# A hybrid decoder layer on one core: transposes one at a time inside the columns, a step more for two chains, and norms' sums kept in written order

## The chip, the core and the metric

The kernel runs on one core of a Trainium2 chip. The metric is device microseconds of one execution. The core's engines work side by side, each through its own instructions in order: PE (TensorE: matmuls, and transposes, which are matmuls with the identity), ACT (ScalarE), DVE (VectorE), POOL (GpSimd) and SP (SyncE). POOL and SP serve here mostly as queues that start DMA transfers. An instruction that waits for another engine holds up everything behind it on its own engine.

## The reference, cut to what matters

The input is 2048 tokens by 1024. One layer is computed in float32:

```
h    = rmsnorm(x) * w1
proj = h @ w_in                       # 3840 columns: 2048 for HGRN2, 1792 for RWKV-7
o_hg = HGRN2 recurrence, 4 heads of 128, each head normed by its mean square, then gated
o_rw = RWKV-7 recurrence, 8 heads of 64 (state S <- S*w + (S a) b' + v k'), group norm, gate
x    = x + concat(o_hg, o_rw) @ w_out
x    = x + conv_ffn(rmsnorm(x) * w2)  # up 1024 -> 5632, causal conv of 3, SiLU gate, down
out  = rmsnorm(x) * w_final
```

## The kernel before

The program has two parts. Part 1 (`phase1`) makes the input projection, both recurrences and most of the output projection; part 2 makes the feed-forward network and the final norm. Every large matmul is made three times on operands split into a high and a low half (L270 to L272, tile `pj` in part 1). What stands in part 2 is not touched here.

Part 1 is written as three Python generators that are advanced in turn:

- `rw_stream` goes through eight RWKV supers (`rw_super`: one block of 512 tokens, two pairs of heads). In a super, PE makes the products of keys and receptances (L730), DVE takes them into `M`, a DMA turns them round through DRAM into `E`, and DVE then solves 31 dependent rows (L802 and L804) and transposes the result into `TZ` (L808). Only then can PE go on: L821, L834 and L847 complete the inverse, ACT copies L847's result out into `UV` and `M`, L867 and L881 prepare the states, and eight steps of L905 and L910 carry the state through the block. A group norm ends the super.
- `hg_stream` goes through sixteen HGRN units (`hg_unit`: one block, one head). At a unit's end PE makes the output (L1064 and L1065), ACT squares it and makes its high half, DVE the low half (`part`), and PE sums both halves over the head (`add_up`, L1083 and L1084, tile `hg`).
- `dense` makes the projection: 30 columns of 128 outputs per block, each of 8 steps k of three matmuls into one of two PSUM banks (`pj`). At a column's end its function takes the result out of the bank: for HGRN one ACT and at most one DVE instruction, for RWKV one ACT and three DVE (L313 to L315). Between columns stand jobs: `load4` loads four rows' tiles (`xt`, one buffer) by SP, `norm4` computes their norm on ACT (`nsq`: squares and sums; `nst`: logarithm and exponential) and DVE, and a transposing job turns the 8 slices of 128 features. Job "T" (`turn`) does so for the next block of x, three times in all; job "N" for block 0 and 1 of the first residual, for the second norm, and stores to `h2d` in DRAM. Each transposed slice takes a `pj` bank, and ACT empties it. `sum_load` and `sum_make` form sums of blocks of `h2d` (`four_sums`, L240 to L243) for part 2; `o_take` brings in halves of an output block. `out_block` makes the output projection of a block.

The pace is set by `fill`: in each round the two streams make one step (to their next `yield`), and then `dense` is advanced for as many nanoseconds, by its own yields, as the constant allows:

```
TICK = 2000.0
        while any(alive.values()):
            for key, g in (("r", rw_), ("h", hg_)):
                ...
                        next(g)
            fill(TICK)
```

A step k of a column is charged 648 ns, a transposed slice 436 ns. The order that results is a priority. A scheduler then places the instructions on each engine by it and by when it reckons that inputs are there and banks are free, so an instruction can stand earlier or later than written. Weights are split while they arrive and kept in DRAM (`Win`) for the later blocks.

Of the kernel before, what the change touches and what calls it, by code (L numbers as in the profile page):

```python
# [7 lines left out]
F32 = mybir.dt.float32  # L8
# [3 lines left out]
AF = mybir.ActivationFunctionType  # L12
# [6 lines left out]
P = 128  # L19
T = 2048  # L20
D = 1024
KD = D // P
BLK = 512
# [44 lines left out]
def tile_layer(ctx, tc, consts, x, norm1_w, w_in, hg_lb_logits, hg_norm_w, rw_shift_mu, rw_w0, rw_w2,  # L68
# [4 lines left out]
    V, S, TE = nc.vector, nc.scalar, nc.tensor  # L73
    dma, store = nc.sync.dma_start, nc.gpsimd.dma_start
# [11 lines left out]
    ident = cp.tile([P, P], F32, name="ident")  # L86
# [27 lines left out]
    def act(out_, in_, func, **kw):  # L114

        want = tables.get(func)
        if want is not None and want != tab["now"]:
            pre = S.preload_act_table_set(want)
            for u_ in tab["uses"]:
                tc.add_manual_dep(pre.ins, u_.ins.name, NOSYNC, reason="table order")  # L120
            tab.update(now=want, pre=pre, uses=[])
        i_ = S.activation(out_, in_, func, **kw)  # L122
        if want is not None:
            tc.add_manual_dep(i_.ins, tab["pre"].ins.name, NOSYNC, reason="table order")
            tab["uses"].append(i_)
        return i_
# [13 lines left out]
    with tc.tile_pool(name="vp", bufs=1, reuse_waits="tile") as vp, tc.tile_pool(name="ps0", bufs=1, space=PSUM, reuse_waits="tile") as pools["ps"]:  # L140
        rows = vp.tile([P, P], F32, name="rows")
# [17 lines left out]
    def vec(nm, i):  # L159
        return vt[:, off[nm] + i:off[nm] + i + 1]  # L160
# [24 lines left out]
    x1d = [dp.tile([BLK, D], F32, name=f"x1d{b}") for b in range(NBLK)]  # L185
    h2d = [dp.tile([D, BLK], F32, name=f"h2d{b}") for b in range(NBLK)]
# [50 lines left out]

    def four_sums(b11, b12, b21, b22):

        V.tensor_sub(b11, b12, b11)  # L240
        V.tensor_sub(b12, b22, b12)
        V.tensor_sub(b22, b22, b11)
        V.tensor_sub(b21, b21, b22)  # L243
        return b11, b22, b12, b21

    def split_to(hi, lo, src):
        c_ = S.copy(hi, src)
        return c_, V.tensor_sub(lo, src, hi.bitcast(F32))
# [9 lines left out]
    def transposed(xt, nm, psum, evict):  # L258

        n = len(xt)  # L260
        for k in range(KD):
            tp = psum()
            for i in range(n):
                TE.transpose(tp[:, i * P:(i + 1) * P], xt[i][:, k * P:(k + 1) * P], ident)
            evict(k, tp[:, :n * P], vec(nm, k))
            yield 109 * n

    def mm3(acc, lhs, rhs, first, last, skip=False):
        (lh, ll), (rh, rl) = lhs, rhs
        TE.matmul(acc, lh, rh, start=first, stop=False, skip_group_check=skip)  # L270
        TE.matmul(acc, lh, rl, start=False, stop=False, skip_group_check=skip)  # L271
        TE.matmul(acc, ll, rh, start=False, stop=last, skip_group_check=skip)  # L272

    def phase1(c1):
# [22 lines left out]
        def bank(kind):  # L297
            return ps.tile([P, 512], F32, tag=kind, name=kind, bufs=2)
# [121 lines left out]
        def load4(key, src, r0):  # L420
            def f():
                rows[key] = row_tile()
                for i in range(4):
                    dma(rows[key][:, i, :], src[r0 + i * P:r0 + (i + 1) * P, :])
            return f

        def norm4(key):
            def f():
                for i in range(4):
                    t_ = rows[key][:, i, :]  # L430
                    V.tensor_scalar_mul(t_, t_, rstd(wp, t_, "nst", "wraw", 4))
            return f

        def four_tiles(t_):
            return [t_[:, i, :] for i in range(4)]

        def turn(nb):

            t_ = rows[nb]
            for k in range(KD):  # L440
                tp = bank("pj")
                for i in range(4):
                    TE.transpose(tp[:, i * P:(i + 1) * P], t_[:, i, k * P:(k + 1) * P], ident)
                act(t_[:, :, k * P:(k + 1) * P], tp.rearrange("p (i t) -> p i t", i=4), AF.Copy)
                yield 436

        def split_h(nb, k):

# [25 lines left out]
        def o_take(m):  # L474

            def f():
                if m == 0:
                    t_ = xp_.tile([P, 2, 2, 4, 256], F32R, tag="xt", name="ohl", bufs=1)
                    rows["O"] = [[t_[:, c, i] for i in range(2)] for c in range(2)]
                t_ = wp.tile([P, 2, 256], F32, tag="wraw", name="oraw", bufs=4)  # L480
                dma(t_, oT[2][2 * m * P:2 * (m + 1) * P, 0:256].rearrange("(k p) t -> p k t", p=P))
                ks = slice(2 * (m % 2), 2 * (m % 2) + 2)
                split_to(rows["O"][0][m // 2][:, ks, :], rows["O"][1][m // 2][:, ks, :], t_)
            return f

        def to_h(k, tp, w):
            act(hh[:, k, :], tp, AF.Copy, scale=w)
            V.scalar_tensor_tensor(hl[:, k, :], tp, w, hh[:, k, :].bitcast(F32), ALU.mult, ALU.subtract)

        def to_h2(nb):  # L490
            def evict(k, tp, w):
                t_ = wp.tile([P, BLK], F32, tag="wraw", name="h2", bufs=4)
                act(t_, tp, AF.Copy, scale=w)
                dma(h2d[nb][k * P:(k + 1) * P, :], t_)
            return evict

        def constants():

# [17 lines left out]
        def dense():  # L516
# [26 lines left out]
            extra = []  # L543
            for nb in range(NBLK):
                if nb + 1 < NBLK:
                    extra += [(at[nb] + 18, ("E", load4(nb + 1, x[0], (nb + 1) * BLK))),
                              (at[nb] + 22, ("E", norm4(nb + 1))), (at[nb] + 25, ("T", nb + 1))]
                if nb >= 2:
                    extra += [(at[nb] + 6, ("E", load4(("N", nb - 2), x1d[nb - 2], 0))),
                              (at[nb] + 10, ("E", norm4(("N", nb - 2)))), (at[nb] + 11, ("N", nb - 2))]  # L550
            for m in range(2):
                extra += [(at[3] + 14 + 5 * m, ("E", sum_load(m))), (at[3] + 17 + 5 * m, ("E", sum_make(m)))]
            extra += [(at[3] + 25 + m, ("W", 2, o_take(m))) for m in range(4)]
# [24 lines left out]
            i = 0  # L578
            load(0)
            ahead = iter(())  # L580
            for n, jb in enumerate(jobs):
                if jb[0] == "E":
                    jb[1]()
                    continue
                if jb[0] == "A":
                    if jb[1] == 0:
                        banks = spread()
                        ahead = transposed(four_tiles(rows[0]), "n1", lambda: next(banks), to_h)
                    continue
                if jb[0] == "T":  # L590
                    yield from turn(jb[1])
                    continue
                if jb[0] == "N":
                    yield from transposed(four_tiles(rows.pop(jb)), "n2", lambda: bank("pj"), to_h2(jb[1]))
                    continue
                if jb[0] in "OW":
                    while done["rw2"] < 2 * jb[1] + 2 or done["hg"] < 4 * jb[1] + 4:
                        yield None
                    if jb[0] == "W":
                        jb[2]()  # L600
                    else:
                        yield from (out_block(2, *rows["O"]) if jb[1] == 2 else out_block(jb[1], then=jb[1] + 2))
                    continue
                _, col, ev, cond, fin = jb
                while not cond():
                    yield None
                load(i)
                ws = loaded.pop(i)
                if i == 0:
                    next(ahead)  # L610
                    next(ahead)
                    constants()
                load(i + 1)
                i += 1
                acc = bank("pj")
                then = jobs[n + 1][1] if jobs[n + 1][0] == "A" else None
                for k in range(KD):
                    wh, wl = ws[k // 4]
                    next(ahead, None)
                    mm3(acc, (wh[:, k % 4, :], wl[:, k % 4, :]), (hh[:, k, :], hl[:, k, :]), k == 0, k == KD - 1)  # L620
                    if k == KD - 1:
                        ev(acc)
                        if fin is not None:
                            fin()
                    next_block(then, k)
                    yield 648

        def last_dma(nb):

# [17 lines left out]
        def rw_super(nb, s_):  # L647
# [6 lines left out]
            def tile_(tag, shape, name):  # L654
                return rp.tile([P] + shape, F32, tag=tag, name=name)
# [200 lines left out]
            for e in range(2):  # L856
                r0, c0 = er0(e), col0(1, e)
                act(M[r0:r0 + 64, 0, 1, :, :, 0:64], quv[1][c0:c0 + 64, :, :, 0:64], AF.Copy)
            yield
            XH = tile_("XH", [2, 9, 64], "XH")  # L860
            V.tensor_copy(XH[:, :, 0, :], Xc[:, 2 * s_:2 * s_ + 2, :])
            xp = bank2()
# [81 lines left out]
        def hg_unit(nb, j):  # L944
# [122 lines left out]
            act(sq, op, AF.Square)  # L1067
            hi, lo = (rp.tile([P, BLK], F32R, tag=tag, name="part") for tag in ("Sf", "VT"))
            split_to(hi, lo, sq)
            yield  # L1070
            ms = bank("hg")
            add_up(ms, ones, hi, lo)
# [552 lines left out]
```

## Time and profile before

| | us |
|---|---|
| median of 3 runs (lowest, highest) | 2640.78 (2636.36, 2642.07) |
| the profiled execution | 2641.65 |
| its span, first to last instruction | 2639.9 |
| part 1, to the first matmul of the last output block, about | 1303 |
| part 2 | 1337 |
| PE busy over the span | 2551.4 |
| DVE, ACT, POOL busy | 1963.1, 1371.3, 381.4 |

The profiled execution stands 0.87 above the median, so a sum worked out against it is read against the median with that difference. Times inside the trace count from the start of the span. The listed duration of a matmul is longer than its pace: those of 512 columns are listed at 0.39 and start every 0.23, since they overlap in the array. A gap is counted from the end of the one before, so it is smaller than what was lost by some 0.16. "PEclk" is the share of the full clock that was granted to PE.

### The profile page before, as it was taken

The page shows a single profiled execution, that of the slowest core. Times are in us where ns is not written, and L with a number is a line of the kernel's source. Part 1 is how long each engine was busy: PE and PEld are TensorE (multiplying, and loading weights), DVE is VectorE, ACT ScalarE, POOL GpSimd, SP SyncE. Part 2 cuts the span into 40 slices and gives each one's busy share as a digit, 9 for nine tenths or more (in the row PEclk, how much of TensorE's full clock was granted, in tenths as well). Part 3 has the DMA queues.
Part 4 walks back from the last instruction along what each step waited for, and adds up shares of the span by engine and source line. Part 5 has one row for each costly group of instructions (what it writes and reads, how often), then busy time and mean ns, then how long its engine had stood idle before and what let it go on. Part 6 is the DMA issues. An engine that isn't in the chain of part 4 may idle for free.

```text
span 2639.9 us, 51054 instructions
## 1 busy us (share of the span) xinstructions
PE 2551.4 (97%) x19467; PEld 2046.3 (78%) x19467; DVE 1963.1 (74%) x3744; ACT 1371.3 (52%) x2258; POOL 381.4 (14%) x686
## 2 busy tenths in 40 slices
PE   7999999989999999999899999999999999999998
PEld 6877777767777767777678888877888888888887
DVE  4878676685666765777687799987998887766556
ACT  5565443555545555345466754456454544545444
POOL 6433222212222122222100000000000000000000
PEclk9999999999999999999999999999999999999999
DMA  8846463646645566845674477746763553998655
GB/s 305 240 153 193 157 176 110 149 149 216 193 168 145 158 211 187 277 145 149 204 253 134 130 235 255 235 158 217 239 207 129 174 169 132 332 321 283 200 190 187
DMA packets 380298, 518.98 MB, mean 197 GB/s; under 512 B 114463, under 2 KB 211093, under 8 KB 380053
## 3 DMA queue, kind: packets, MB, share of 16 engines
q1 hardware_dynamic: 325521, 337.38, 40.2%
q0 software_dynamic: 54464, 178.32, 21.0%
q8 instruction: 153, 2.51, 0.4%
q14 instruction: 92, 0.75, 0.1%
q10 hardware_dynamic: 68, 0.02, 0.0%
HBM read 372.99 MB, written 134.22 MB: 192 GB/s over the span
## 4 chain that ended last, share of the span: by engine, by line
PE 69%; DVE 13%; ACT 7%; DMA 7%; issue 4%; POOL 0%; SPq 0%; DVEq 0%; ACTq 0%; POOLq 0%
PE pj L270 7%; PE pj L271 7%; PE pj L272 7%; PE ua L270 4%; PE ua L272 4%; PE ua L271 4%; PE da L270 3%; PE da L271 3%; PE da L272 3%; PE ud L271 2%; PE ud L270 2%; PE ud L272 2%; PE db L272 2%; PE db L271 2%; PE db L270 2%
## 5 line engine op out<-in xcount | busy, mean ns | idle before, releaser
L270 PE MATMUL pj<-hh,wh 128*128 128x512 f32 x960 | 392.2, 409 | 4.5 <-ACT rkv L122 2.5
L271 PE MATMUL pj<-hl,wh 128*128 128x512 f32 x960 | 378.4, 394 | 0.0
L272 PE MATMUL pj<-hh,wl 128*128 128x512 f32 x960 | 378.3, 394 | 0.0
L270 PE MATMUL ua<-Bh,uwh 128*128 128x512 f32 x704 | 276.8, 393 | 3.0 <-ACT m L122 2.5
L272 PE MATMUL ua<-Bh,uwl 128*128 128x512 f32 x704 | 274.5, 390 | 0.0
L271 PE MATMUL ua<-Bl,uwh 128*128 128x512 f32 x704 | 274.2, 389 | 0.0
L270 PEld LDWEIGHTS pj<-hh,wh 128*128 128x128 f32 x960 | 181.2, 189 | 53.5 <-issue 8.3
L272 PEld LDWEIGHTS pj<-hh,wl 128*128 128x128 f32 x960 | 181.3, 189 | 39.5 <-issue 0.2
L271 PEld LDWEIGHTS pj<-hl,wh 128*128 128x128 f32 x960 | 181.3, 189 | 35.3 <-issue 0.6
L254 ACT CAST uwh<-uraw 128x512 fp32r<-128x512 f32 x220 | 134.2, 617 | 131.0 <-PE ua L271 54.0
L255 DVE TENSOR_TENSOR dal<-draw,dah 128x512 fp32r<-128x512 f32 x138 | 95.2, 690 | 110.9 <-ACT dah L254 108.5
L255 DVE TENSOR_TENSOR uwl<-uraw,uwh 128x512 fp32r<-128x512 f32 x220 | 147.1, 684 | 32.8 <-ACT uwh L254 32.7
L254 ACT CAST dah<-draw 128x512 fp32r<-128x512 f32 x138 | 85.8, 622 | 164.2 <-PE da L271 77.8
L270 PEld LDWEIGHTS ua<-Bh,uwh 128*128 128x128 f32 x704 | 132.3, 188 | 34.8 <-ACT m L122 7.0
L272 PEld LDWEIGHTS ua<-Bh,uwl 128*128 128x128 f32 x704 | 132.3, 188 | 28.1 <-DVE uwl L255 0.4
L271 PEld LDWEIGHTS ua<-Bl,uwh 128*128 128x128 f32 x704 | 132.2, 188 | 26.6
L1495 POOL DMA_DIRECT2D gd<-y x2 | 1.1, 540 | 949.0 <-DVE y L1493 949.0
L270 PE MATMUL ud<-Bh,uwh 128*128 128x512 f32 x352 | 138.0, 392 | 0.0
L272 PE MATMUL ud<-Bh,uwl 128*128 128x512 f32 x352 | 137.1, 390 | 0.0
L271 PE MATMUL ud<-Bl,uwh 128*128 128x512 f32 x352 | 137.0, 389 | 0.0
L271 PE MATMUL da<-dbl,dah 128*128 128x512 f32 x332 | 129.5, 390 | 0.2 <-DVE dbl L255 0.2
L272 PE MATMUL da<-dbh,dal 128*128 128x512 f32 x332 | 129.2, 389 | 0.0
(582 smaller groups left out, 6202.6 us busy)
## 6 DMA issues: line engine op xcount, KB each, us to landing
uraw<-in_w_up_dram SPq DMA_DIRECT2D x176, 256.0 KB, 3.2
woraw<-in_w_out_dram POOLq DMA_DIRECT2D x96, 256.0 KB, 3.6
br<-gd SPq DMA_DIRECT2D x88, 256.0 KB, 4.3
draw<-Sg SPq DMA_DIRECT2D x88, 256.0 KB, 3.0
draw<-Tw SPq DMA_DIRECT2D x88, 256.0 KB, 3.2
gd<-y SPq DMA_DIRECT2D x86, 256.0 KB, 3.0
Sg<-br SPq DMA_DIRECT2D x72, 256.0 KB, 2.5
xt<-x1d SPq DMA_DIRECT2D x32, 512.0 KB, 6.2
```

The source lines that it names most:

```text
L254: S.copy(hi, src)
L255: V.tensor_sub(lo, src, hi.bitcast(F32))
L270: TE.matmul(acc, lh, rh, start=first, stop=False, skip_group_check=skip)
L271: TE.matmul(acc, lh, rl, start=False, stop=False, skip_group_check=skip)
L272: TE.matmul(acc, ll, rh, start=False, stop=last, skip_group_check=skip)
L1495: (dma if end is None else nc.gpsimd.dma_start)(gd_[2 * h + b][fb * P:(fb + 1) * P, :], ys[0][:, b * BLK:(b + 1) * BLK])
```

## The change

Four edits, all in part 1:

1. `four_sums`: its first subtraction is tied behind whatever DVE instruction is written before it. The same is done to the two instructions of each split in `o_take`.
2. `turn` becomes a job per slice. The slices are put on a list, and a column takes one from it after its matmuls of k = 1 and one after k = 5; the step that does so is charged 648 + 436. For the next block the slices are spread one per column over eight columns (from column 22), for the second norm two per column over four (`turn2`, from column 8). The loads and norms ahead of them move to column 17 and 20 (before 18 and 22), and 4 and 7 (before 6 and 10).
3. `rw_super` has one `yield` more between ACT's copies out of L847 and the states (L867).
4. `hg_unit` has one more between the split and the sum (L1083).

```diff
-        V.tensor_sub(b11, b12, b11)
+        tc.keep_in_program_order(V.tensor_sub(b11, b12, b11))
...
-        def turn(nb):
-
-            t_ = rows[nb]
-            for k in range(KD):
+        def turn(nb, k):
+
+            def f():
+                t_ = rows[nb]
                 tp = bank("pj")
                 for i in range(4):
                     TE.transpose(tp[:, i * P:(i + 1) * P], t_[:, i, k * P:(k + 1) * P], ident)
                 act(t_[:, :, k * P:(k + 1) * P], tp.rearrange("p (i t) -> p i t", i=4), AF.Copy)
-                yield 436
+            return f
+
+        def turn2(key, k):
...
+                h2 = wp.tile([P, BLK], F32, tag="wraw", name="h2", bufs=4)
+                act(h2, tp, AF.Copy, scale=vec("n2", k))
+                dma(h2d[key[1]][k * P:(k + 1) * P, :], h2)
...
-                split_to(rows["O"][0][m // 2][:, ks, :], rows["O"][1][m // 2][:, ks, :], t_)
+                for i_ in split_to(rows["O"][0][m // 2][:, ks, :], rows["O"][1][m // 2][:, ks, :], t_):
+                    tc.keep_in_program_order(i_)
...
-                    extra += [(at[nb] + 18, ("E", load4(nb + 1, x[0], (nb + 1) * BLK))),
-                              (at[nb] + 22, ("E", norm4(nb + 1))), (at[nb] + 25, ("T", nb + 1))]
+                    extra += [(at[nb] + 17, ("E", load4(nb + 1, x[0], (nb + 1) * BLK))),
+                              (at[nb] + 20, ("E", norm4(nb + 1)))]
+                    extra += [(at[nb] + 22 + k, ("T", turn(nb + 1, k))) for k in range(KD)]
                 if nb >= 2:
-                    extra += [(at[nb] + 6, ("E", load4(("N", nb - 2), x1d[nb - 2], 0))),
-                              (at[nb] + 10, ("E", norm4(("N", nb - 2)))), (at[nb] + 11, ("N", nb - 2))]
+                    extra += [(at[nb] + 4, ("E", load4(("N", nb - 2), x1d[nb - 2], 0))),
+                              (at[nb] + 7, ("E", norm4(("N", nb - 2))))]
+                    extra += [(at[nb] + 8 + k // 2, ("T", turn2(("N", nb - 2), k))) for k in range(KD)]
...
                 if jb[0] == "T":
-                    yield from turn(jb[1])
+                    turns.append(jb[1])
                     continue
...
                     mm3(acc, (wh[:, k % 4, :], wl[:, k % 4, :]), (hh[:, k, :], hl[:, k, :]), k == 0, k == KD - 1)
+                    aside = k in (1, 5) and len(turns) > 0
+                    if aside:
+                        turns.pop(0)()
...
-                    yield 648
+                    yield 648 + 436 * aside
...
                 act(M[r0:r0 + 64, 0, 1, :, :, 0:64], quv[1][c0:c0 + 64, :, :, 0:64], AF.Copy)
             yield
+            yield
             XH = tile_("XH", [2, 9, 64], "XH")
...
             split_to(hi, lo, sq)
             yield
+            yield
             ms = bank("hg")
             add_up(ms, ones, hi, lo)
```

In the changed kernel, lines of `rw_super` stand 9 or 10 further down (L821 is L830, L867 is L877), those of `hg_unit` 10 or 11 (L1083 is L1094). How the order moves at three places:

PE where block 2 of x is transposed, at about 490 us (L443 are the transposes of x, a row's `x12` is three slices; L1083 and L1084 are the sums of RWKV's norms). Before:

```order
L272 MATMUL pj<-hh,wl 128x512
L443 MATMUL pj<-ident,xt 128x128 x12
L1083 MATMUL rw<-part,group 128x512
L443 MATMUL pj<-ident,xt 128x128 x12
L1084 MATMUL rw<-part,group 128x512
L1083 MATMUL rw<-part,group 128x512
L1084 MATMUL rw<-part,group 128x512
L443 MATMUL pj<-ident,xt 128x128 x8
L270 MATMUL pj<-hh,wh 128x512
```

And one of the eight slices now:

```order
L270 MATMUL pj<-hh,wh 128x512
L271 MATMUL pj<-hl,wh 128x512
L272 MATMUL pj<-hh,wl 128x512
L443 MATMUL pj<-ident,xt 128x128 x4
L1094 MATMUL rw<-part,group 128x512
L1095 MATMUL rw<-part,group 128x512
L1094 MATMUL rw<-part,group 128x512
L1095 MATMUL rw<-part,group 128x512
L270 MATMUL pj<-hh,wh 128x512
```

The eight slices stood in one run with only the sums between; now each stands alone between a column's matmuls.

DVE in block 3, where the second of the two `four_sums` stood (L240 to L243, tile `xt`; the rest are HGRN's levels and norm, and L887 is RWKV's, for which L881's second half waits). Before:

```order
L1076 TENSOR_TENSOR osq<-hg,osq 128x512
L240 TENSOR_TENSOR xt<-xt 128x1024
L1077 TENSOR_TENSOR hgg<-osq,hgg 128x512
L947 TENSOR_SCALAR hk<-hf 128x512
L974 TENSOR_TENSOR hf<-hf 128x256
L971 TENSOR_TENSOR hX<-hk,Sf 128x128x2
L965 TENSOR_TENSOR hX<-hq,hf 128x128x2
L972 TENSOR_TENSOR Sf<-Sf,hf 128x128x2
L241 TENSOR_TENSOR xt<-xt 128x1024
```

Now the first `four_sums` stands at this place, whole, and the second one comes only after all eight state steps:

```order
L240 TENSOR_TENSOR xt<-xt 128x1024
L241 TENSOR_TENSOR xt<-xt 128x1024
L242 TENSOR_TENSOR xt<-xt 128x1024
L243 TENSOR_TENSOR xt<-xt 128x1024
L968 MEMSET Sf 128x256
L313 SCALAR_TENSOR_TENSOR rkv_13102<-pj,vt,rkv_13102 128x511
L1087 TENSOR_TENSOR osq<-hg,osq 128x512
```

The sums moved as a group, and none is left ahead of RWKV's additions.

ACT at the start of block 2 (and, alike, of block 3), where the second norm's rows are squared as they arrive (`nsq`) and the first columns' results are taken out (`tl`, `rkv`). Before:

```order
L122 ACTIVATE nsq,nst<-xt 128x1024
L122 ACTIVATE tl<-pj,omu 128x512
L122 ACTIVATE nsq,nst<-xt 128x1024
L122 ACTIVATE tl<-tl 64x512
L122 ACTIVATE nsq,nst<-xt 128x1024 x2
L122 ACTIVATE rkv_7891<-pj,omu 128x512 x2
L122 ACTIVATE rkv_7966<-pj,omu 128x512
```

Now:

```order
L122 ACTIVATE tl<-tl 64x512
L118 ACT_TABLE_LOAD
L122 ACTIVATE nst<-nst,eps_71 128x1 x2
L122 ACTIVATE nst<-nst 128x1
L122 ACTIVATE nsq,nst<-xt 128x1024
L122 ACTIVATE nst<-nst 128x1
L122 ACTIVATE rkv_7895<-pj,omu 128x512
L122 ACTIVATE nst<-nst,eps_71 128x1
L122 ACTIVATE nsq,nst<-xt 128x1024
```

The first RWKV result is now taken out before the fourth square instead of after it, and the norm's logarithm and exponential, with a load of ACT's function table, came in between. The order has 61 such loads in the whole program where it had 53; those of part 2 are the same. From the last matmuls of part 1 on, PE, DVE and ACT have the same instructions in the same order as before.

More of the change, by code (lines that the diff above doesn't have):

```diff
@@ L444, in turn, with f @@
                 act(t_[:, :, k * P:(k + 1) * P], tp.rearrange("p (i t) -> p i t", i=4), AF.Copy)
-                yield 436
+            return f
+        def turn2(key, k):
+            def f():
+                t_ = rows[key]
+                tp = bank("pj")
+                for i in range(4):
+                    TE.transpose(tp[:, i * P:(i + 1) * P], t_[:, i, k * P:(k + 1) * P], ident)
+                h2 = wp.tile([P, BLK], F32, tag="wraw", name="h2", bufs=4)
+                act(h2, tp, AF.Copy, scale=vec("n2", k))
+                dma(h2d[key[1]][k * P:(k + 1) * P, :], h2)
+            return f
         def split_h(nb, k):
@@ L488, in to_h @@
             V.scalar_tensor_tensor(hl[:, k, :], tp, w, hh[:, k, :].bitcast(F32), ALU.mult, ALU.subtract)
[L490 to L495, printed above, removed]
         def constants():
@@ L580, in dense @@
             ahead = iter(())
+            turns = []
             for n, jb in enumerate(jobs):
@@ L590, in dense @@
                 if jb[0] == "T":
-                    yield from turn(jb[1])
-                    continue
-                if jb[0] == "N":
-                    yield from transposed(four_tiles(rows.pop(jb)), "n2", lambda: bank("pj"), to_h2(jb[1]))
+                    turns.append(jb[1])
                     continue
```

## The prediction

> **What bounds the kernel now.** I read the page's engine totals first, then the two parts as windows of their own, PE's waits, the places where its clock fell, and the timeline around each of the four edits.
>
> ```profile
> span 2639.9 us, 51054 instructions
> PE 2551.4 (97%) x19467; PEld 2046.3 (78%) x19467; DVE 1963.1 (74%) x3744; ACT 1371.3 (52%) x2258; POOL 381.4 (14%) x686
> ```
>
> The windows' columns are length, busy time of PE, PE's weight loads, DVE, ACT and POOL (instructions), PE's clock, DMA share, GB/s. The first is part 1, the second part 2.
>
> ```profile
> 0.00:1303.00 1303.00, 1233.67 (x13666) 965.09 (x13667) 906.91 (x2148) 663.95 (x1116) 365.54 (x657) 0.99 0.60 182
> 1303.00:2640.00 1337.00, 1317.73 (x5803) 1081.24 (x5802) 1056.21 (x1597) 707.30 (x1143) 15.81 (x29) 1.00 0.64 210
> ```
>
> PE is the bound in both, and the work on it is the same after the change. Part 2 keeps its order, so the change can reach only the 1303.00 − 1233.67 = 69.3 us in which PE stands in part 1, the clock there, and new waits. The waits that the edits touch (engine, line, releaser: us in all, times, longest):
>
> ```profile
> PE hg L1084 <- DVE part L248: 5.3, 8, 1.8
> PE rw L881 <- DVE AR L887: 4.2, 1, 4.2
> PE rw L867 <- ACT M L122: 4.1, 7, 2.1
> PE pj L443 <- ACT hf L122: 4.1, 2, 2.1
> ...
> PE rw L821 <- DVE TZ L808: 2.9, 5, 1.0
> ```
>
> Together they are 20.6 of PE's 69 us. The clock adds to it: in four windows of 3.4 us it was 0.50, each at or within about 2 us behind one of these waits, so each cost half of 3.4 = 1.7 us more. A fifth window, behind a wait of 2.52, had the full clock.
>
> ```profile
> 214.90:218.30 3.40, 3.40 (x14) 2.90 (x14) 3.40 (x4) 2.87 (x7) 1.91 (x4) 0.50 0.67 227
> 416.30:419.70 3.40, 3.40 (x9) 2.31 (x7) 0.98 (x3) 3.28 (x7) 0.19 (x1) 0.50 0.50 159
> 761.00:764.40 3.40, 3.30 (x55) 3.14 (x57) 3.23 (x9) 1.80 (x4) 0.00 (x0) 0.50 0.02 5
> 1109.20:1112.60 3.40, 3.40 (x23) 2.30 (x14) 1.92 (x4) 0.07 (x1) 1.07 (x2) 0.50 0.44 161
> 987.00:990.40 3.40, 3.38 (x15) 2.81 (x16) 0.85 (x3) 0.00 (x0) 0.31 (x1) 1.00 0.13 53
> ```
>
> There is a second bound in places. Summed over the eight windows in which DVE solves RWKV's 31 rows (L802 to L808), DVE is busy 223.72 of 241.20 us, 93%, and PE arrives at L821 within a microsecond of DVE's transpose in most of them. The seventh:
>
> ```profile
> sum 241.20, PE 229.62 PEld 183.34 DVE 223.72 ACT 124.43 POOL 65.94; mean PE 28.70 PEld 22.92 DVE 27.96 ACT 15.55 POOL 8.24
> 1085.77 1.03 DVE L808 STREAM_TRANSPOSE TZ<-Ti 128x512 f32<-128x512 f32 x1
> 1086.85 0.75 PE L821 MATMUL rw<-TZ,M 32*32 32x32 f32 x64 [0.74 <-DVE TZ L808]
> ```
>
> So PE's time saved inside such a window may come back as a wait at L821; time saved outside it counts.
>
> **The change part by part.** Bounds stand in brackets, gains negative, all against the profiled 2641.65.
>
> *HGRN's extra step.* The sum (L1083, L1084) moves later on PE, past about 2 us more of matmuls by the order; nothing is added. The largest case now:
>
> ```profile
> 414.15 0.50 PE L1084 MATMUL hg<-part,ones 128*128 128x512 f32 x1 [1.84 <-DVE part L248]
> ...
> 415.29 0.75 PE L821 MATMUL rw<-TZ,M 32*32 32x32 f32 x64
> ```
>
> This gap is real, since nothing holds L821 behind it, and the drop at 416.30 follows it: 1.84 + 1.7 = 3.5. The other seven waits are 5.3 − 1.84 = 3.5 together; several lie in DVE's windows and two units still have little ahead of the sum, so I count none of them. **−3.5** [0 if later work only waits in its stead; −7.0 with all waits and the drop]. Its HGRN head ends some 2 us later; its store and the output projection that needs it stand far behind.
>
> *RWKV's extra step.* PE's work between L847 and L867 grows from about 2.5 us to 2.7 to 4.6 by the order. What is waited for is ACT's copies:
>
> ```profile
> 760.42 1.82 ACT L122 ACTIVATE M<-rw 128x512 f32<-128x512 f32 x3
> 761.07 3.85 PE L867 MATMUL rw<-UV,KBT 128*64 128x64 f32 x64 [2.06 <-ACT M L122]
> ```
>
> All of L867's 4.1 and the drop at 761.00, 1.7, are 5.8; a unit with only 2.7 of cover keeps some of its wait. **−5** [0; −5.8].
>
> *The sums in written order.* Now one `four_sums`, begun early, is spread over the state's preparation, and its third instruction stands ahead of what L881 needs:
>
> ```profile
> 1105.70 1.22 DVE L242 TENSOR_TENSOR xt<-xt 128x1024 f32<-128x1024 f32 x1
> ...
> 1107.43 0.68 DVE L887 TENSOR_TENSOR AR<-rw,AR 128x512 f32<-128x512 f32 x1
> ...
> 1108.26 0.69 PE L881 MATMUL rw<-M 64*64 64x64 f32 x32 [4.17 <-DVE AR L887]
> ```
>
> With no sum left there the wait of 4.17 and the drop at 1109.20, 1.7, go. DVE has no other instruction longer than these at this place; what is late next is the second `four_sums`, 4 × 1.22 = 4.9 us of DVE at the super's end (a rival below). **−5.5** [0; −5.9]. `o_take` orders splits whose readers come blocks of work later: nothing, hidden by the columns.
>
> *The second norm earlier.* At block 3's start ACT squares the last row, just arrived, ahead of the first RWKV result (the order above), and PE waits for that:
>
> ```profile
> 985.14 1.25 ACT L122 ACTIVATE rkv<-pj,omu 128x512 f32<-128x512 f32 x2
> 987.02 0.47 PE L270 MATMUL pj<-hh,wh 128*128 128x512 f32 x1 [2.52 <-ACT rkv L122]
> ```
>
> Now that result is taken out first, but a table load and the norm's short instructions have come in ahead of it. **−1.5** [−2.5 for the whole wait; +2.6 for two loads in the open, row below].
>
> *The transposes.* Five runs of 32 transposes become 40 slices among columns. Two runs from first transpose to next column:
>
> ```profile
> 210.96 0.60 PE L443 MATMUL pj<-ident,xt 128*128 128x128 f32 x4
> 213.54 0.66 PE L443 MATMUL pj<-ident,xt 128*128 128x128 f32 x4 [1.98 <-ACT hf L122]
> ...
> 220.84 0.50 PE L270 MATMUL pj<-hh,wh 128*128 128x512 f32 x1 [0.20 <-ACT xt L122]
> 489.68 0.60 PE L443 MATMUL pj<-ident,xt 128*128 128x128 f32 x4
> ...
> 498.11 0.50 PE L270 MATMUL pj<-hh,wh 128*128 128x512 f32 x1 [0.25 <-ACT xt L122]
> ```
>
> Needed are 32 × 0.13 (eight in 1.04 us where they ran freely) + 4 sums × 0.23 = 5.1. The first run took 9.9, the second 8.4: 4.8 (1.7 of it the clock's) and 3.3 lost. The other three I put at 2.5 each: 15.6 in all to be had. Against it stands what a slice waits inside a column. A slice needs the bank that the column before used, and it comes behind as little as six matmuls of the next, 6 × 0.23 = 1.4 us. What empties that bank (us in all, mean ns; then idle time ahead), and ACT's table load:
>
> ```profile
> L118 ACT ACT_TABLE_LOAD x53 | 68.0, 1283 | 1.7 <-PEq L1610 0.7
> L122 ACT ACTIVATE rkv<-pj,omu 128x512 f32<-128x512 f32 x48 | 32.8, 685 | 130.5 <-PE pj L272 130.4
> L313 DVE SCALAR_TENSOR_TENSOR rkv<-pj,vt,rkv 128x511 f32<-128x511 f32 x48 | 35.8, 747 | 57.8 <-ACT rkv L122 57.5
> ```
>
> Behind an RWKV column that is 0.69 + 2 or 3 × 0.75, about 2.5 us, so 1.1 more than the six matmuls cover; behind an ACT-only column 0.6 to 1.1, covered. By the order 8 slices stand behind an RWKV column, 11 behind one with two instructions, 13 behind ACT alone and 8 behind another slice, most with more than six matmuls between. My estimate of the mean waits, 0.6, 0.35, 0.2 and 0.27 for the four kinds, gives 4.8 + 3.9 + 2.6 + 2.2 = 13.5, about 14 with ends. Net **−2** [−15.6 if all is covered; 32 × 1.1 − 15.6 = +19.6 if each of the first three kinds waits like the worst].
>
> *DVE's windows and SP.* By the order's instructions at the trace's mean durations, both DVE's and PE's work inside the eight windows falls by some 7 us, so their balance stays. In two supers a store of `h2d` now stands on SP between the stores and loads that turn `M` round, and waits for a slice: some 1.5 us each at worst outside cover. **+1** [−3; +5].
>
> *Table loads.* Eight more, 8 × 1.283 = 10.3 us of ACT, which is busy half of the time, so most is hidden; a quarter in the open is **+2.5** [0; +10.3].
>
> Sum: −3.5 − 5 − 5.5 − 1.5 − 2 + 1 + 2.5 = −14.0, so 2641.65 − 14.0 = **2627.6**. The median stands 0.87 lower than the profiled run, which is inside what I can tell: no change is anything within 0.2%, 5.3 us, so 2635.5 to 2646.
>
> **The rivals.**
>
> *DVE's loop keeps its length.* If the 31 rows last as long as before with 7 us less PE work beside them, PE waits 7 more at L821; the two SP stores cost 3 rather than 1; half of the HGRN gain lies there and goes, 1.7. −14.0 + 7 + 2 + 1.7 = −3.3: 2638.4, no change to tell. For it speaks the 93% and the near ties at L821; against it, that the DVE work taken out stands in the same queue as the rows, and should shorten the loop.
>
> *The clock drops stay.* The wait of 2.52 us that ends at 987.02 had no drop behind it, so a drop isn't tied to a wait's length alone. With those at 214.90, 416.30 and 761.00 kept or put elsewhere, 3 × 1.7 = 5.1 are not gained: 2632.7. [...]
>
> *The slices wait for their banks.* If ACT and DVE have a queue at the columns' ends, 32 slices wait 1.1 as behind the worst column, 35 instead of 14, +21; and the gaps, forty short ones, drop the clock four times more, +6.8. 2627.6 + 27.8 = 2655.4, slower. It decides once the mean wait of a slice is over 0.7 us, 28 in 40: then the edits' other gains are used up. For it: two banks only, and DVE busy 93% in the windows in which some of the slices fall. Against: the order leaves 1.4 to 5.9 us of matmuls ahead of each. [...] No drop in this trace stands in a run of columns without a longer gap, so I give it no more.
>
> *The second `four_sums` blocks the super's end.* Its 4.9 us of DVE ahead of RWKV's norm reach PE: 2632.5. Against: HGRN's columns and units stand there for PE.
>
> **How the numbers follow.** My case 0.53, DVE's loop 0.18, the clock 0.08, the slices 0.15, the second sum 0.06. My case's own range is 2618 to 2635, the root of the squares of the terms' spreads on the side of their likelier ends, about 8. The range goes to 2613, where the transposes reach their good end (13.6 further), and to 2645, which takes in the loop's rival and a slice wait of 0.7 and leaves out most of the slower one: **2613 to 2645**. Faster by over 0.2%: 0.53 + 0.08 + 0.06, 0.67; within: 0.18 and a little of the others, 0.19; slower: 0.14.
>
> **What the profile after would show.** Right: no wait at L877 (L867 before), L1095's (L1084) down to about 2 us, none of 4 us at the states of block 3; no run of transposes with gaps of 2 us; waits of L443 and L453 and of the columns behind them near 14 us; at most one window at 0.50. Wrong: those waits at 28 or more; L830's (L821) at 8 or more instead of 2.9; ACT's table loads as releasers of PE's waits.

## The result and the profile after

Median of the change 2636.65 us, of the kernel before 2642.06, 20 runs each; ratio 0.9978 (0.9971 to 0.9986). One of the change's 20 runs took 4858.63 us; it counts as slow and is not in the ratio. The change is 5 to 6 us faster, 3.7 to 7.7 by the interval. The prediction was 13 faster. Its time stood in the range and its sign was right, but less than half of the gain came.

The change's page:

```profile
span 2637.6 us, 51053 instructions
PE 2545.3 (97%) x19467; PEld 2046.8 (78%) x19467; DVE 1968.2 (75%) x3744; ACT 1384.5 (52%) x2266; POOL 381.7 (14%) x686
```

Its two parts as windows, columns as before:

```profile
0.00:1301.00 1301.00, 1227.62 (x13666) 962.53 (x13667) 911.88 (x2148) 675.59 (x1124) 365.56 (x657) 0.99 0.60 183
1301.00:2637.60 1336.60, 1317.72 (x5802) 1084.23 (x5802) 1056.29 (x1597) 708.87 (x1143) 16.14 (x30) 0.99 0.64 210
```

Part 1 is 2 us shorter, and part 2 as long as before. In part 1 PE is busy 6 us less for the same number of matmuls (why is not worked out here), but it stands 73.4 us (1301.00 − 1227.62) where it stood 69.3. The waits that the edits aimed at did go. PE's waits in part 1, of the change (L1095 was L1084, L877 was L867, L891 was L881, L830 was L821, L1094 was L1083; L1000 and L1075, before L990 and L1065, are HGRN's products; L443 and L453 are the slices):

```profile
PE hg L1000 <- issue: 3.9, 3, 1.5
...
PE rw L830 <- DVE TZ L817: 3.6, 4, 1.1
PE rw L891 <- DVE AR L897: 3.4, 4, 1.3
...
PE hg L1075 <- DVE SH L1067: 3.3, 3, 1.7
...
PE hg L1000 <- DVE hk L957: 2.1, 1, 2.1
...
PE pj L270 <- ACT nsq L122: 1.7, 1, 1.7
...
PE rw L877 <- ACT M L122: 1.6, 3, 1.3
PE pj L270 <- ACT xt L122: 1.5, 1, 1.5
...
PE pj L443 <- DVE hgg L370: 1.5, 1, 1.5
PE hg L1094 <- ACT part L247: 1.3, 1, 1.3
...
PE pj L453 <- ACT h L122: 0.8, 2, 0.4
PE pj L453 <- DVE hq L346: 0.7, 2, 0.4
...
PE hg L1095 <- DVE part L248: 0.2, 1, 0.2
PE pj L443 <- DVE hq L346: 0.2, 1, 0.2
```

HGRN's sum went from 5.3 to 0.2 (its first matmul waits 1.3, before 0.4), the states from 4.1 to 1.6, the single wait of 4.2 became four short ones, and the 40 slices with the column behind one of them wait 4.7 in all (1.5 + 1.5 + 0.8 + 0.7 + 0.2). So time came back at places that the prediction had not priced. HGRN's own products are one: L1000 waits 6.0 us where L990 waited 0.3, L1075 3.3 where L1065 waited 1.3. Two more are plain in the trace. One is the fourth super's DVE loop, at about 524 us, here before and after:

```profile
524.10:559.10 35.00, 30.69 (x404) 23.88 (x402) 30.85 (x110) 19.11 (x35) 6.08 (x11) 1.00 0.56 158
```

```profile
523.70:565.50 41.80, 32.83 (x433) 25.84 (x432) 35.16 (x116) 22.81 (x40) 5.36 (x10) 0.91 0.59 157
```

The other is the crossing into part 2, whose first matmuls (`wacc`) take the last output block. PE and then DVE in the change:

```profile
1298.33 0.39 PE L272 MATMUL pj<-wh,hl 128*128 128x512 f32 x1
1300.87 1.36 PE L1281 MATMUL wacc<-woh,Bh 128*128 128x512 f32 x4 [2.15 <-ACT Bh L247]
1302.67 2.08 PE L1281 MATMUL wacc<-wol,Bh 128*128 128x512 f32 x4 [0.44 <-DVE wol L248]
1308.36 2.07 PE L1281 MATMUL wacc<-woh,Bl 128*128 128x512 f32 x4 [3.61 <-DVE Bl L248]
1300.14 0.68 DVE L1088 TENSOR_TENSOR hgg<-osq,hgg 128x512 f32<-128x512 f32 x1
...
1307.61 0.69 DVE L248 TENSOR_TENSOR Bl<-uraw,Bh 128x512 fp32r<-128x512 f32 x1 [5.00 <-DMA oT<-hgg]
```

The window behind the first of these waits:

```profile
1301.70:1311.90 10.20, 6.15 (x14) 3.98 (x13) 5.20 (x10) 3.47 (x7) 1.44 (x3) 0.50 0.88 299
```

The last HGRN product (`hgg`) is made about 1.5 us after PE had run out of matmuls, and is finished 2 us after. It goes through DRAM, and PE waits 6.2 us in three pieces; the third, 3.61, is for this way. The first ends when both the product and ACT's first `Bh` are done, within 0.01 us of each other, so the trace cannot tell which of them it was. The clock stands at 0.50 for 10.2 us. Before, the product was made 4 us ahead of PE's last columns' end, and the one wait over a microsecond there was 2.14, at full clock:

```profile
1298.16 0.68 DVE L1077 TENSOR_TENSOR hgg<-osq,hgg 128x512 f32<-128x512 f32 x1
...
1301.48 1.22 DVE L938 TENSOR_TENSOR yo<-rw,yo 128x1024 f32<-128x1024 f32 x1
1302.89 1.17 PE L1270 MATMUL wacc<-woh,Bh 128*128 128x512 f32 x4
...
1311.97 0.50 PE L1270 MATMUL wacc<-woh,Bl 128*128 128x512 f32 x1 [2.14 <-DVE Bl L248]
```

From the first `wacc` on the order is the same in both kernels, but not just ahead of it. On DVE `hgg` stood ahead of RWKV's last addition (`yo`, L938); now it stands behind it (L948, at 1299.01).

### The profile page after: what moved, and what is told of

Read it like the earlier page. It is cut to its first block, busy times and chain, and to the rows that moved or that the text cites. A ratio compares the mean times of both kernels' runs of the same rounds, so it can differ in the third digit from the quotient of the medians.

```text
span 2637.6 us, 51053 instructions
## 1 busy us (share of the span) xinstructions
PE 2545.3 (97%) x19467; PEld 2046.8 (78%) x19467; DVE 1968.2 (75%) x3744; ACT 1384.5 (52%) x2266; POOL 381.7 (14%) x686
## 4 chain that ended last, share of the span: by engine, by line
PE 53%; issue 7%; DVE 6%; DMA 5%; ACT 4%; POOL 1%; SPq 0%; DVEq 0%; POOLq 0%; ACTq 0%
PE ua L270 5%; PE ua L272 5%; PE ua L271 5%; PE pj L270 3%; PE da L271 3%; PE da L270 3%; PE da L272 3%; PE ud L271 3%; PE pj L271 3%; PE ud L270 3%; PE ud L272 3%; PE pj L272 3%; PE db L271 2%; PE db L272 2%; PE db L270 2%
```

## The experiments

Each kernel is compared with runs of the kernel before on the same chip. Differences in us are the ratio's, on 2641.

**Each edit by itself.** Four kernels, each with the kernel before and one edit's lines of the diff.

> Only the transposes are taken into the columns (with the loads and norms ahead of them); the other three edits are left out. Theory 1 (the missing gain was lost in the DVE loop of super 4 and in clock drops that the slices bring there): about 2645, +2 to +6 against before, with a lower mean clock than before. Rival 2 (the four terms are true and the loss comes only when all four stand together): the prediction's term alone, -2, so about 2640. Rival 3 (each edit deals the order anew, and what it gains at its own place is noise beside that): anything from -8 to +8, with no sum that fits.

> Only HGRN's extra step. Theory 1 and rival 2: -3.5 (0 to -7), PE's waits at the sum's second matmul down from 5.3 to about 2 us and the drop at 416 us gone. Rival 3: the waits go, and the time moves by some other number of either sign, since windows elsewhere change.

> Only RWKV's extra step. Theory 1 and rival 2: -5 (0 to -5.8), the waits at the first product of the states down from 4.1 to under 1 us. Rival 3: the waits go, the time moves by another number.

> Only the sums and the output splits in written order. Theory 1 and rival 2: -5.5 (0 to -5.9), the wait of 4.17 us in block 3 and the drop behind it gone. Rival 3: the wait goes, the time moves by another number.

| | median | ratio (95%) | us |
|---|---|---|---|
| slices, with the norms ahead of them | 2637.60 | 0.9987 (0.9977 to 0.9997) | −3.4 |
| HGRN's step | 2648.61 | 1.0029 (1.0017 to 1.0040) | +7.7 |
| RWKV's step | 2644.14 | 1.0011 (1.0000 to 1.0021) | +2.9 |
| sums in written order | 2632.10 | 0.9968 (0.9957 to 0.9980) | −8.5 |

By the ratio the sums alone do better than all four edits together, though the two intervals meet. Their trace runs beside that of before until 1085 us, and then, in block 3, the states' preparation has no wait:

```profile
1100.63 0.69 DVE L885 TENSOR_TENSOR M<-rw,cst 128x512 f32<-128x512 f32 x1 [1.43 <-PE rw L882]
1101.24 0.68 DVE L888 TENSOR_TENSOR AR<-rw,AR 128x512 f32<-128x512 f32 x1
1101.98 0.75 DVE L313 SCALAR_TENSOR_TENSOR rkv<-pj,vt,rkv 128x511 f32<-128x511 f32 x1
...
1103.76 0.69 DVE L885 TENSOR_TENSOR M<-rw,cst 128x512 f32<-128x512 f32 x1 [0.71 <-PE rw L882]
```

DVE now waits for PE where PE waited 4.17 us for DVE, and no cold window (a stretch with PE's clock at 0.50) follows.

The two steps, alone, are no gain. With HGRN's step its own sum's wait fell as foreseen, but RWKV's norm, which uses the same two lines (tile `rw`), waited instead:

```profile
PE rw L1084 <- ACT part L247: 6.8, 7, 2.0
...
PE rw L1085 <- DVE part L248: 3.4, 4, 1.4
...
PE hg L1085 <- DVE part L248: 0.9, 1, 0.9
```

10.2 us, where before the two had 2.0 and 2.6. In the first two blocks every second HGRN unit's sum stands 11 to 13 us later than before (at 206.9 for 195.6, 350.6 for 337.8), where RWKV's sums around it are 2 to 6 later. So it comes nearer to those of RWKV's norm sums that wait, at 216 to 219 and at 361. With RWKV's step the states' wait fell from 4.1 to 0.8 and the time did not fall. In the slices' trace the wait that the sums cause grew from 4.17 to 6.76, so part of the slices' gain may have been hidden behind it; the two edits together, below, do not bear this out.

Theory 1, that the slices cost, fell. Rival 2 held for slices and sums and not for the steps.

**Is it the round, or the later sum?** An extra step gives a unit one round more. So the round was given without the later sum, and the later sum without the round:

```diff
+            yield                 # ahead of the sum (hgrn_moved) ...
             ms = bank("hg")
...
             done["hg"] += 1
-            yield                 # ... and one less at the unit's end
```

`hgrn_end_step` instead has a second `yield` after that line; `rwkv_moved` has RWKV's step and none at its super's end; `sums_slices` has two edits of the change whole.

> HGRN's extra step ahead of the sum as in the change, but the step at the unit's end is taken out, so that a unit has as many steps, and the streams as many rounds, as before. Theory P (the extra step costs by its round: 16 rounds more shift the streams against the columns everywhere, and the new meetings cost more than the sum gains): the waits at the sum go and the time is -3.5 against before, 2636 to 2640. Rival L (the later sum itself costs: HGRN's norm and what follows it comes late): as with the extra step, +5 to +8, so 2647 to 2650.

> No step ahead of the sum; instead one step more at the end of each HGRN unit, where nothing waits, so the streams have the same 16 rounds more. Theory P: slower like the extra step itself and by its lost gain more, +5 to +12. Rival L: no change, -2 to +2.

> RWKV's extra step ahead of the states, and the step at the super's end taken out, so the steps of a super are as many as before. Theory P: -3 to -6 (the prediction's -5 without the price of eight rounds). Rival L: as with the extra step, +2.

> The sums in written order and the slices in the columns, without the two extra steps. If the edits add up: -9.9 and -4.3 of the single runs, so about -14 at best, 2627 to 2631, and faster than all four together by 6 or more. Rival (the edits take the same time away): 2632 to 2637, no faster than the sums alone.

| | median | ratio (95%) | us |
|---|---|---|---|
| `hgrn_moved` | 2653.28 | 1.0052 (1.0033 to 1.0071) | +13.7 |
| `hgrn_end_step` | 2640.69 | 0.9999 (0.9988 to 1.0009) | −0.3 |
| `rwkv_moved` | 2659.53 | 1.0066 (1.0047 to 1.0084) | +17.4 |
| `sums_slices` | 2631.50 | 0.9965 (0.9952 to 0.9977) | −9.2 |

Theory P fell: sixteen rounds more cost nothing by themselves that can be told. They also brought 61 loads of ACT's table where before had 53, so eight more loads came at no cost that can be told. Rival L is nearer, but does not explain why taking the end's step away made both moved kernels worse than the extra step alone; that stays open. And the slices add next to nothing to the sums: 0.9965 against 0.9968.

**One edit less, and smaller pieces.** `all_but_hgrn` and `all_but_rwkv` are the change less that one `yield`; `sums_without_splits` ties the subtraction only; in `hgrn_one_step` one unit has the step:

```diff
             split_to(hi, lo, sq)
             yield
+            if (nb, j) == (1, 0):
+                yield
```

> The change without HGRN's extra step. If that step costs in company what it costs alone (+6.7): 2628 to 2632, 5 to 8 below the change. Rival (it costs alone because HGRN's later units meet RWKV's norm sums where the run of transposes stands; with the slices spread that meeting is gone, and the step is free or a gain): within 2 of the change, 2634 to 2638.

> The change without RWKV's extra step. If that step costs in company as alone (+2.2): 2633 to 2635. Rival (what the change gives back in super 4's loop and at the end of part 1 comes of this step): 2628 to 2632, and the loop of super 4 back from 42 us to about 35.

> Only the first subtraction of the sums of blocks is kept in written order; the splits of the output halves are left as before. The prediction costed the splits at nothing: then the same as the edit whole, 2631 to 2634, some 8 to 10 under before. Rival (the part of the gain beyond the predicted 5.5 is the splits'): 5 to 6 under before.

> HGRN's extra step in one unit alone, the one that waited 1.84 us at 414 us; fifteen are as before. Theory (the price of a wait is the local one, and the loss of the whole edit comes of the other units' being moved): -2 to -4 against before. Rival (any move deals the rest anew): the wait goes, and the time moves by -4 to +6 from other places.

| | median | ratio (95%) | us |
|---|---|---|---|
| the change without HGRN's step | 2634.17 | 0.9975 (0.9964 to 0.9986) | −6.6 |
| the change without RWKV's step | 2622.68 | 0.9935 (0.9921 to 0.9949) | −17.2 |
| sums without the splits | 2632.42 | 0.9973 (0.9962 to 0.9983) | −7.1 |
| HGRN's step in one unit | 2640.49 | 1.0004 (0.9993 to 1.0016) | +1.1 |

RWKV's step is where the gain went: without it the change is 11.4 us faster still (17.2 − 5.8), the fastest kernel of all here. HGRN's step is neutral beside RWKV's (0.9975 against 0.9978), and a gain of 7.9 us without it (0.9935 against 0.9965 for sums and slices alone). Read the other way, RWKV's step costs 2.9 us alone and 2.6 beside sums and slices (0.9975 against 0.9965, whose intervals meet), and 11.4 only where HGRN's step is there too: the two steps act on each other. Why HGRN's step gains here what it lost alone is open. The splits are worth nothing that can be told. In the one unit the wait fell from 1.84 to 0.28, a cold window came nevertheless (at 420.2, before at 416.3), and the time stayed.

**Where RWKV's step is paid.** With the step the fourth loop was 40.7 to 42.6 us long in three traces, and 30.0 to 37.0 in the ten that leave RWKV's steps alone. So the step was divided, `if 2 * nb + s_ >= 3:` ahead of the extra `yield`, and `< 3`.

> All four edits, but RWKV's extra step only from the fourth super on; the fourth's own step stands behind its loop. If the step costs because it sets the first supers back, so that more of block 0's output projection (24 matmuls of it in the loop without the step, 41 to 58 with it) and its splits fall into the fourth super's loop: loop of about 31 us, 24 or so of these matmuls in it, and 2622 to 2627, near the 2622.7 of the change without the step. Rival (the step costs something in every super): between, 2628 to 2632. Rival (the later ones cost, at the end of part 1): 2632 to 2637.

> All four edits, but RWKV's extra step only in the first three supers. If the fourth super's loop is where the step costs: loop of about 41 us, 40 or more of these matmuls in it, and 2630 to 2636. Rival (something in every super): 2626 to 2629. Rival (the later ones): 2622 to 2626.

2634.58, ratio 0.9982 (0.9973 to 0.9990), −4.8; and 2624.97, ratio 0.9944 (0.9931 to 0.9957), −14.8. My theory fell outright. With the step from the fourth super on the loop is 31.2 us long, as the theory asked, and the gain is lost nevertheless. With the step in the first three supers the loop is as long as in the change, and the time is good:

```profile
524.10:564.70 40.60, 32.81 (x433) 25.61 (x433) 35.21 (x116) 22.69 (x41) 5.35 (x10) 0.92 0.56 157
```

So 6 us of a lengthened loop are made up: block 2's first column starts at 631.3 us, and at 631.0 in the change without RWKV's step. The later supers cost. In both traces of the good kernels the crossing has none of the waits above; the trace of `step_from_fourth` has them (2.13, 0.59 and 4.32). The change without RWKV's step, PE and DVE:

```profile
1283.68 0.39 PE L272 MATMUL pj<-wh,hl 128*128 128x512 f32 x1
1283.91 1.16 PE L1280 MATMUL wacc<-woh,Bh 128*128 128x512 f32 x4
1284.90 1.07 PE L1280 MATMUL wacc<-wol,Bh 128*128 128x512 f32 x4
1286.35 1.20 PE L1280 MATMUL wacc<-woh,Bl 128*128 128x512 f32 x4 [0.38 <-DVE Bl L248]
1282.13 0.69 DVE L1087 TENSOR_TENSOR hgg<-osq,hgg 128x512 f32<-128x512 f32 x1
```

The last product is made at 1282, ahead of the last output matmuls' end, and not behind it. Hence three kernels on the last super: the step everywhere but there (`< 7`), the step there alone (`== 7`), and the change whole with no extra step in the last HGRN unit.

> All four edits, but no extra step in the last RWKV super. If the step's cost is the crossing into part 2 (the last super's norm meets the last HGRN unit's on ACT and DVE, the last product is stored late, and part 2's first matmuls wait 5.8 us and run cold): no wait of 2 us or more at part 2's first matmuls, 2625 to 2629. Rival (supers 4 to 7 cost as well, a few us each): 2629 to 2635.

> All four edits, with RWKV's extra step in the last super alone. If the crossing is the cost: waits at part 2's first matmuls as in the change, 2628 to 2634, that is 6 to 11 above the change without the step. Rival: 2622 to 2625, no wait there.

> The change whole, with RWKV's step, but no extra step in the last HGRN unit, so that its sum stands earlier than RWKV's norm. If the meeting of the two norms is what costs at the crossing: the wait for the last product is gone or down to 2 us, 2629 to 2634. Rival (RWKV's tail itself is what part 2 waits for): no change, 2634 to 2638.

| | median | ratio (95%) | us |
|---|---|---|---|
| RWKV's step not in the last super | 2626.11 | 0.9943 (0.9926 to 0.9959) | −15.1 |
| in the last super alone | 2629.30 | 0.9954 (0.9937 to 0.9971) | −12.1 |
| no HGRN step in the last unit | 2634.93 | 0.9973 (0.9962 to 0.9984) | −7.1 |

Taken away from the last super alone, the step's cost goes: 9.2 of the 11.4 us, with intervals that do not touch the change's. That one `yield` moves this much is shown. PE's recorded order is the same in both kernels up to 1236.3 us of the change's trace, 1230.9 of the other's, so the order differs only from about there on; of the 13.5 us between the two ends (2637.6 and 2624.1) 8.1 come behind that point. In the last super alone the step costs 5.0 by the ratios (0.9954 against 0.9935, whose intervals meet), about half of the 9.2, and its trace has the crossing's waits again, one after the other:

```profile
1291.11 1.19 PE L1282 MATMUL wacc<-woh,Bh 128*128 128x512 f32 x4 [2.14 <-DVE hgg L1089]
1292.92 1.94 PE L1282 MATMUL wacc<-wol,Bh 128*128 128x512 f32 x4 [0.61 <-DVE wol L248]
1299.22 1.22 PE L1282 MATMUL wacc<-woh,Bl 128*128 128x512 f32 x2 [4.36 <-DVE Bl L248]
```

The crossing is thus where the trace shows it. In this trace block 3's 27th column starts 1.7 us later than in the change without RWKV's step (1170.83 for 1169.15) and the program ends 11.6 later (2630.4 for 2618.8), so some 10 us come behind that column. These are single executions, though. Over the 19 traces part 2 took between 1330.7 and 1340.6 us from its first `wacc`, with its order untouched. So the traces show where the waits stand, and the medians what the step costs.

That the two norms' meeting makes the cost is not shown. Without HGRN's last step the profiled run, one of the two fastest of its kernel, has one wait over 0.2 us at the first `wacc`, of 1.41, and that is for RWKV's last addition (`yo`). The median of 2634.93 is no lower than the change's beyond the intervals and lies in the rival's range, by which RWKV's own tail is what part 2 waits for. The traces agree with that rival in part: RWKV's last addition ends 3.5 to 3.9 us ahead of the first `wacc` in the three kernels whose last super has no extra step, 0.6 ahead in the change and with the step in the last super alone, and 1.8 behind it without HGRN's last step. What holds up the other runs of that kernel is open.

## Why the prediction missed

**The step that failed.** It is the term for RWKV's extra step: −5 in the sum, +11.4 measured in the company of the other edits, 9.2 of it by the last of eight supers. The sum's other terms come to −9.0 (−14.0 + 5), and the change without that step measured −17.2. So the total missed by two errors that partly cancel, and that the time still lay in the range owes something to luck.

**The bound.** Right that PE bounds part 1 and that part 2's order is untouched. The sentence "Part 2 keeps its order, so the change can reach only" PE's standing time and clock in part 1, "and new waits" names new waits, but the sum has no term for any at part 2's first matmuls. Their inputs are made at the end of part 1, and these came later: 6.2 us of waits and 10.2 at half clock. Set against before, part 2 is no longer in the two profiles (1336.6 us from 1301 on, and 1336.9 from 1303 on before, where it had a wait near its start too). The loss shows in the medians, against the kernels that have no step in the last super.

**HGRN's step, −3.5.** Alone +7.7; in the change nothing that can be told; without RWKV's step −7.9 (0.9935 against 0.9965). The waits went as worked out. What failed is "Its HGRN head ends some 2 us later; its store and the output projection that needs it stand far behind." Alone, every second unit of the first two blocks came 11 to 13 later, towards RWKV's norm; and behind the last unit's store stood part 2.

**RWKV's step, −5.** Alone +2.9; in the change +11.4. The waits of L867 did fall, to 1.6. I had priced the one wait ahead of the states and nothing of what follows them: each state, norm and store of that super also comes later, and for the last super little is left to cover it. Some 2 us of the 11.4 the last super does not explain; the waits of L1000, 6.0 in the change, are absent without RWKV's step, but that they are this cost is not shown. Without the step the wait for the states is 3.8, nearly that of before, and that kernel is the fastest.

**The sums, −5.5.** Right in place and mechanism, and in size as far as can be told: −8.5 whole and −7.1 without the splits, and both intervals take in −5.5. The rival of the second `four_sums` had no sign in it.

**The slices, −2, and the norm, −1.5.** Together −3.4 measured (−6 to −1 by the interval), which is the sum of these two terms; but with +1 and +2.5 for the windows and the loads I had put the group at nothing. The size of a part was off: I took 14 us for the waits of 40 slices, and the trace shows 4.7. By the prediction's estimate of what the runs lost, 15.6 − 4.7 = 11 are won at the place, and most of that does not arrive at the end; beside the sums next to none does. The norm's wait fell from 2.52 to 1.7. The rival of slices that wait for their banks fell: the fastest kernel has all 40 slices. No run shows its +6.8, four more drops from forty short gaps: part 1 of the change has five stretches at half clock, 27.3 us together, and before had five of 20.4; which of them the slices made is not shown.

**The loads, +2.5.** Eight more loads came, `hgrn_end_step` has as many at no cost that can be told, and the fastest kernel has 63, ten more than before: the term is about 0.

**The loop of DVE.** The rival "DVE's loop keeps its length" gave too much to a single loop. The fourth one lengthened by 6.8 us and PE waited in it, and such a loop is made up later, as the first-three kernel shows.

**The clock.** The price was probably too high. 3.4 us at half clock I took as 1.7 of PE's pace (in the window of before from 1266.2 on, matmuls of 512 columns start 0.43 us apart instead of 0.23), but over the 24 runs of before beside the first four experiments a mean clock lower by 0.001 goes with 1.4 us more, where a full 0.001 of 2640 is 2.6. By that a cold window costs about 1.7 × 1.4 / 2.6 = 0.9. Runs of before beside the other experiments give 1.0 to 2.2 instead of 1.4, so this is rough. The sign "at most one window at 0.50" failed: the change's part 1 has five such stretches and the crossing a sixth. And whether a wait has a drop behind it differed between two executions, as the last section shows, so the four drops that I counted as removed were no sure gain.

## What to carry to other kernels

Price a moved step to the end of its chain, not to the wait that it removes: look first at the last instance of the chain, where nothing stands behind it as cover, and at what the next stage takes from it. A wait removed in the middle of a stage with slack elsewhere can be worth little or nothing (1.84 us gone in one unit changed nothing that can be told, 6 us more in one loop were made up). One instance at a crossing between stages was worth 9.2 us here. And when several edits are made together, run them each alone and each left out: here one of four took back two thirds of what the other three gained, and alone it cost only 2.9.

## What the runs showed of the hardware

The cold windows of before in part 1 start at 214.9, 416.3, 761.0, 1109.2 and 1266.2; the last of these the prediction had overlooked. Four are 3.4 us long and the last 6.8. In the 3.4 us ahead of them PE was busy for 0.94 to 2.15:

```profile
211.50:214.90 3.40, 1.14 (x6) 0.61 (x5) 3.40 (x6) 3.37 (x6) 0.66 (x2) 1.00 0.20 77
412.90:416.30 3.40, 2.15 (x69) 1.61 (x70) 3.22 (x10) 1.74 (x3) 0.87 (x2) 0.99 0.02 8
757.60:761.00 3.40, 1.41 (x9) 0.91 (x7) 3.40 (x7) 3.33 (x8) 0.00 (x0) 1.00 0.20 77
1105.80:1109.20 3.40, 0.94 (x61) 0.97 (x64) 3.40 (x5) 0.00 (x0) 0.00 (x0) 0.99 0.66 249
1262.80:1266.20 3.40, 1.91 (x36) 1.40 (x36) 2.95 (x9) 2.23 (x7) 0.00 (x0) 1.00 0.81 235
```

In the first of these rows PE's waits are 1.98 (up to 213.54) and 0.28. About the same wait can have a drop behind it or none: that of PE at the start of block 3 (2.52 us before, 2.44 with the sums edit) shows both. The 3.4 us that hold most of it and the next, before and then with the sums:

```profile
982.90:986.30 3.40, 1.60 (x8) 0.98 (x6) 0.46 (x1) 2.21 (x4) 1.32 (x3) 1.00 0.71 225
986.30:989.70 3.40, 2.68 (x12) 2.24 (x13) 1.52 (x6) 0.09 (x1) 0.00 (x0) 1.00 0.36 140
```

```profile
982.40:985.80 3.40, 0.96 (x5) 0.49 (x3) 1.22 (x4) 2.30 (x4) 1.07 (x2) 0.99 0.80 259
985.80:989.20 3.40, 3.40 (x8) 2.65 (x9) 0.75 (x3) 0.00 (x0) 0.00 (x0) 0.50 0.18 71
```

PE was busy 1.60 us of the first stretch before and 0.96 with the sums; the one trace stayed at full clock and the other went to half. What decides it is not shown. So about the same wait had a drop behind it in one execution and none in another, and the clock of a single profile is no basis for a price.
